# Projecting the values of one attention group with the weights stationary and turning them afterwards

## The chip, the cores and the metric

The kernel runs on one core of a Trainium2 chip. Times are device microseconds (us) of that core. Engines are called as in the profile: PE (TensorE, its weight loads shown apart as PEld), DVE (VectorE), ACT (ScalarE), POOL (GpSimd) and SP (SyncE, whose queue here issues the DMAs).

## What is computed

One layer of a hybrid trunk on 512 tokens of width 1024: a norm, one projection `w_in` that feeds four mixers (pooling, dilated attention, stick-breaking attention, an S5 state space branch), gates, an output projection, and a gated feed-forward layer. The change touches dilated attention, which has three groups of four heads of 64; group `g` attends among tokens at distance 1, 4 and 16:

```
proj = rmsnorm(x, g) @ w_in                       # [512, ...]
for g, (window, dil) in enumerate(((128, 1), (512, 4), (2048, 16))):
    # tokens r, r + dil, r + 2 dil, ... form a subsequence of their own
    s = q @ k.T / 8 + bias[bucket(distance)]      # banded, causal, per subsequence
    m = max(s); p = exp(s - m); den = sum(p)
    o[g] = (p @ v) / den;  lse[g] = m + log(den)
y = sum(softmax(lse over g)[g] * o[g])
```

In group 1 (dilation 4) there are four subsequences of 128 tokens. The product `p @ v` of one of them wants its 128 tokens of `v` on the partitions, with the head dimension along the row.

## The kernel before

Everything is kept transposed, features on the 128 partitions and the 512 tokens along the row. Each fp32 operand of a large product is split into a rounded high part and a remainder (`split`, and `split_next` for weights), and a product takes three matmuls: high by high, high by low, low by high.

The work is one main stream of products, written out in the order in which PE gets it, with weight chunks that are loaded on SP's queue (`load_next`), split in halves by ACT and DVE (`split_next`, one chunk ahead of its use) and then multiplied. Two forms of product occur. `mm3` holds a 128 x 128 block of weights stationary and moves all 512 tokens past it; eight k tiles by three make 24 matmuls, and the result is transposed (features on partitions). `act_stationary` holds 128 tokens of the input stationary and moves 256 columns of weights, again 24 matmuls; its result has the tokens on the partitions.

The projections of dilated attention are made in a loop over `g` = 0, 1, 2: queries, keys, values, two heads' worth (128 features) at a time for queries and keys. Tokens of groups 1 and 2 are put in the order of their subsequences when PSUM is evicted (`perm_out`, `perm_in`). For the values, groups 0 and 1 use `act_stationary` on four blocks of tokens: 128 neighbours in group 0, every fourth token, `slice(b, T, 4)`, in group 1. ACT evicts with the norm's per-token scale, a column: `rc[0]`, or `rc[1]`, the same scale in group 1's token order, which is made by a store to DRAM and a load back. Group 2 uses `mm3` twice, evicts on DVE with a permuting write into two `vf` tiles, and turns them later, in `dil_gen`, by eight 128 x 128 transposes on PE into two PSUM tiles `vt` and copies by ACT.

Everything else of the mixers is side work: generators (`s5_gen`, `dil_gen`, `sb_gen`, `pool_gen` and so on) that `start` puts on a list. `tick`, called after each product of the main stream, goes through the list and issues one step of each, in the order of the list. The list pauses a step where a simple account of engine times (`clock`) has DVE or ACT more than `MAX_LAG` = 4 us behind PE. PSUM has three banks for the main stream and five for side work, each in rotation. The order on every engine is thus fixed when the program is built. Around the values of group 1 the steps are: an S5 step and a step of scores after each half of the values, with the split of the next chunk (group 2's queries) before them; then group 2's queries, before which the chunk of its keys is split.

The lines that matter in the program: the loop `for g in range(3)` of the projections, `act_stationary`, `dil_gen`, and

```
if g < 2:
    vt = [slot("v"), slot("v")]
    for b in range(4):
        ps = main_ps("v")
        act_stationary(ps, ch, slice(b * P, (b + 1) * P) if g == 0 else slice(b, T, 4))
```

Of the kernel before, what the change touches and what calls it, by code (L numbers as in the profile page):

```python
# [10 lines left out]
F32 = mybir.dt.float32  # L11
F32R = mybir.dt.float32r
I32 = mybir.dt.int32
AF = mybir.ActivationFunctionType
ALU = mybir.AluOpType
AX = mybir.AxisListType
PSUM = bass.MemoryType.PSUM
DRAM = bass.MemoryType.DRAM

P = 128  # L20
T = 512
# [22 lines left out]
CST_CNT = 512  # L44
CST_W = CST_CNT + 64

N_SLOTS = 61  # [128, 512] tiles in the rotating pool
N_RAW = 2  # weight chunks loaded ahead
N_PM = 3  # PSUM banks of the main stream; the rest serve side work
S5_RATE = 0.9  # steps of the S5 branch per tick  # L50
SB_RATE = 1.0  # steps of the stick-breaking branch per tick
MAX_LAG = 4.0  # backlog of DVE and ACT (us) at which side work pauses
H_WAIT = 4  # ticks between the S5 rotation tables and their use
SB_T = 2  # steps from stick-breaking scores to their transposes
SB_O = 2  # steps from the transposes to the outputs
DIL_O = 1  # the same for the dilated branch
N_WARM = 8  # products on constants that bring up the PE clock while the first loads run
N_HALVED = 2  # last tiles of w_down done by token halves
BC_AT = 7  # k tiles of the last product before the first half is broadcast
W0_PIECES = {0: 1, 1: 3, 4: 2, 6: 2}  # first k tile: number of k tiles, pieces of the first weight chunk  # L60
S5_PAR = 48
S5_W = S5_PAR + 4 * 256

# [25 lines left out]
def hybrid_trunk(ctx: ExitStack, tc: tile.TileContext, a: dict, out: bass.AP):  # L89
    nc = tc.nc  # L90
    G, SY = nc.gpsimd, nc.sync
    clock = {"pe": 0.0, "v": 0.0, "a": 0.0}
# [12 lines left out]
    mixers = ExitStack()  # L105
# [9 lines left out]
    def slot(nm):  # L115
        return sp.tile([P, T], F32, tag="s", name=nm_(nm))
# [8 lines left out]
    def side_ps(nm):  # L125
        return pa.tile([P, T], F32, tag="at", name=nm_("s_" + nm))
# [9 lines left out]
        V.tensor_tensor(r_(lo), src, hi, ALU.subtract)  # L136
        return r_(hi), r_(lo)

    # ------------------------------------------------------- weight stream
    specs = (  # L140
        [("w_in", 17 + c, 2048) for c in range(2)]
        + [("w_in", 2 + 3 * w + g, 2048) for g in range(3) for w in range(3)]
# [21 lines left out]
    loaded, ready = [], []  # L164
# [35 lines left out]
            PE.matmul(ps, wh, al, start=False, stop=False)  # L200
            PE.matmul(ps, wl, ah, start=False, stop=k == n - 1)

    # ------------------------------------------------- side work scheduling
    active = []

    def start(gen, rate=1.0):
        active.append([gen, 0, rate, 0.0])
        return active[-1]
# [19 lines left out]
        while e in active:  # L228
            tick(True)

    # ---------------------------------------------------------------- loads
    ones = gp.tile([P, P], F32, name="ones")
    G.memset(ones, 1.0)
    warm = gp.tile([P, 1], F32, name="warm")
# [45 lines left out]
    def g3(kt):  # L280
        return cols[:, 16 + kt : 17 + kt]

    # ------------------------------------------------------------- rms norm
    def sumsq_add(acc, src):
        sq = slot("sq")
        A.activation(sq, src, AF.Square)
# [5 lines left out]
    def inv_rms(ps, n):  # L292
        def s_(nm):
            return gp.tile([P, n], F32, name=nm_(nm))

        ms = s_("ms")
        V.tensor_scalar(ms, ps, 1.0 / D, EPS, ALU.mult, ALU.add)
        rt = s_("rt")
        A.activation(rt, ps, AF.Sqrt, scale=1.0 / D, bias=epsc)
        r0 = s_("r0")  # L300
        V.reciprocal(r0, rt)
        t = s_("nt")
        V.tensor_tensor(t, r0, r0, ALU.mult)
        V.scalar_tensor_tensor(t, t, -0.5, ms, ALU.mult, ALU.mult)
        r = s_("rr")
        V.scalar_tensor_tensor(r, t, 1.5, r0, ALU.add, ALU.mult)
        return r

    def diags(r, nm):
        o = []  # L310
        for b in range(4):
            dg = sm.tile([P, P], F32, tag="dg", name=nm_("dg"), bufs=4)
            V.tensor_scalar(dg, ident, r[:, b : b + 1], None, ALU.mult)
            o.append(dg)
        return o
# [7 lines left out]
    def ssq_mm(acc):  # L323
        ps = side_ps("ssq")
        for b in range(4):
            PE.matmul(ps[:, b : b + 1], acc[:, b * P : (b + 1) * P], ones[:, 0:1], start=True, stop=True)
        return ps

    # ------------------------------------------------------------- prologue
    xg = []  # L330
    ch0 = Chunk()
    ch0.hi = wp.tile([P, 2048], F32R, tag="hi", name=nm_("hi"))
# [12 lines left out]
    rb8 = slot("rb8")  # L345
    env = {}

    # ------------------------------------------------- relative bias tables
    bias_d = dp.tile([12, BIAS_N], F32, name="bias_d")
    bias = {}  # L350

# [28 lines left out]
                SY.dma_start(bias[g, h], bass.AP(src.tensor, src.offset + off, [[1, P], [1, w]]))  # L380
            off += BIAS_L[g]

    # -------------------------------------------------------- S5 parameters
    s5 = cp.tile([P, S5_W], F32, name="s5p")
    are, aim, ldt = s5[:, 0:16], s5[:, 16:32], s5[:, 32:48]

# [287 lines left out]
            ys5.append(split(yg, "yg"))  # L674
            yield

    # ------------------------------------------------------ dilated attention
    def perm_out(t, g):
        if g == 0:
            return t  # L680
# [33 lines left out]
    def dil_score(g, hp, bl):  # L714
# [14 lines left out]
        for hh in range(2):  # L729
# [15 lines left out]
                )  # L745
            yield

    def dil_gen():
        for g in range(3):
            while len(dk) < 2 * g + 2:  # L750
# [3 lines left out]
                    yield from dil_score(g, hp, bl)  # L754
            if g:
                move(stat_d[g], stats[g].rearrange("p b s h -> p b (s h)"), g, True)
        vt = [slot("v"), slot("v")]
        for hb in range(2):
            ps = side_ps("vt")
            for bb in range(2):  # L760
                b = 2 * hb + bb
                for n in range(2):
                    PE.transpose(ps[:, bb * 256 + n * P : bb * 256 + n * P + P], vfs[n][:, b * P : (b + 1) * P], ident)
            A.copy(vt[hb], ps)
        dv.append(vt)
        yield
        for g in (1, 2):
            move(stat_d[g], nat[g].rearrange("p b s h -> p b (s h)"), 0, False)
        yield 2
# [73 lines left out]
                    V.tensor_scalar(st[:, o : o + kn], st[:, o : o + kn], fw[g][:, b, h : h + 1], None, ALU.mult)  # L843
            yield

    # ------------------------------------------------------- stick breaking
    sq, sk, sv = [], [], []
    m_up = cst[:, CST_UP : CST_UP + P]
    m_low = cst[:, CST_LOW : CST_LOW + P]
# [44 lines left out]
                V.tensor_tensor(be[:, : n - 1], be[:, : n - 1], om[:, 1:n], ALU.mult)  # L894
            yield

    # ----------------------------------------------------------------- pool
    ypool = [None] * 4
    pwt = []

# [33 lines left out]
        V.scalar_tensor_tensor(r_(lo), ps, cols[:, 24 + g : 25 + g], hi, ALU.mult, ALU.subtract)  # L934
        ypool[g] = (r_(hi), r_(lo))

    # ------------------------------------------------------------ main: w_in
    start(bias_tables())
    start(pool_load())
    e_s5 = start(s5_gen(), S5_RATE)  # L940
# [23 lines left out]
            split_next()  # L964
    ch = next_chunk()
    mm3(pss[2], ch, 0, 256, xg)
    rc = [inv_rms(ssq_mm(acc)[:, 0:4], 4), gp.tile([P, 4], F32, name="rc_perm")]
    dgs = diags(rc[0], "r1")
    rc_d = dp.tile([T], F32, name="rc_d")
    SY.dma_start(rc_d.rearrange("(b p) -> p b", b=4), rc[0])  # L970
    SY.dma_start(rc[1], rc_d.rearrange("(p b) -> p b", b=4))
    mm3(pss[3], ch, P, 256, xg)
    bcast_rows(dgs, rb)
    V.tensor_scalar(rb8, rb, 0.125, None, ALU.mult)
# [5 lines left out]
    def act_stationary(ps, ch, tk):  # L980
        for k, (ah, al) in enumerate(xg):
            PE.matmul(ps[:, 0:256], ah[:, tk], ch.h(k, 0, 256, 256), start=k == 0, stop=False)
            PE.matmul(ps[:, 0:256], al[:, tk], ch.h(k, 0, 256, 256), start=False, stop=False)
            PE.matmul(ps[:, 0:256], ah[:, tk], ch.l(k, 0, 256, 256), start=False, stop=k == KT - 1)

    e_dil = start(dil_gen())
    for g in range(3):
        for lst, scale in ((dq, rb8), (dk, rb)):
            ch = next_chunk()
            for n in range(2):  # L990
                ps = main_ps("qk")
                mm3(ps, ch, n * P, 256, xg)
                t = slot("qk")
                V.tensor_tensor(perm_out(t, g), perm_in(ps, g), perm_in(scale, g), ALU.mult)
                lst.append(t)
                tick()
        ch = next_chunk()
        if g < 2:
            vt = [slot("v"), slot("v")]
            for b in range(4):  # L1000
                ps = main_ps("v")
                act_stationary(ps, ch, slice(b * P, (b + 1) * P) if g == 0 else slice(b, T, 4))
                A.activation(
                    vt[b // 2][:, (b % 2) * 256 : (b % 2) * 256 + 256],
                    ps[:, 0:256],
                    AF.Copy,
                    scale=rc[g][:, b : b + 1],
                )
                if b % 2:
                    tick()  # L1010
            dv.append(vt)
        else:
            for n in range(2):
                ps = main_ps("v")
                mm3(ps, ch, n * P, 256, xg)
                t = slot("vf")
                V.tensor_tensor(perm_out(t, g), perm_in(ps, g), perm_in(rb, g), ALU.mult)
                vfs.append(t)
                tick()

    def sb_qk(c):
        for lst in (sq, sk):
# [9 lines left out]
    def sb_v(c):  # L1032
        ch = next_chunk()
        vt = [slot("sv"), slot("sv")]
        for b in range(4):
            ps = main_ps("sv")
            act_stationary(ps, ch, slice(b * P, (b + 1) * P))
            A.activation(
                vt[b // 2][:, (b % 2) * 256 : (b % 2) * 256 + 256], ps[:, 0:256], AF.Copy, scale=rc[0][:, b : b + 1]
            )  # L1040
            if b % 2:
                tick()
        sv.append(vt)
# [18 lines left out]
    sb_v(1)  # L1062
    e_sb = start(sb_gen(), SB_RATE)

    # --------------------------------------------------- gates and branches
    merged = [slot("mg") for _ in range(8)]
    mg = []

# [46 lines left out]
    branch(3, yglu, last=True)  # L1115
    mixers.close()

    # ------------------------------------------------- output of the mixers
    fp = ctx.enter_context(tc.tile_pool(name="ffn", bufs=1))

    def keep(nm):
# [18 lines left out]
            acc = sumsq_add(acc, t)  # L1140
    rb2 = keep("rb2")

    # ------------------------------------------------------------------ ffn
    def glu_up(psg, psu):
        tg, tu = slot("tg"), slot("tu")
        V.tensor_tensor(tg, psg, rb2, ALU.mult)
# [28 lines left out]
            if part:  # L1175
                acc = sumsq_add(acc, x2[nt])

    # ------------------------- the last tiles by token halves, final rms norm
    H = T // 2
    last = [(nt, next_chunk()) for nt in range(8 - N_HALVED, 8)]  # L1180
    pq = [side_ps("ssq"), side_ps("ssq")]
# [201 lines left out]
```

## Time and profile before

| | |
|---|---|
| median of 3 runs | 1000.56 us (1000.35 to 1001.05) |
| span of the profiled execution | 999.0 us |
| PE busy | 986.6 us (99%) |
| PEld busy | 828.5 us (83%) |
| DVE busy | 574.1 us (57%) |
| ACT busy | 361.5 us (36%) |
| DMA | 100.18 MB, mean 100 GB/s |

The page gives the span, from the first to the last instruction, of the one execution that was profiled, and no other time of it; the median is 1.56 us above it. Busy times overlap between engines. The records of all operations carry line 79, that of the helper which issues them, so instructions are told apart by the tiles that they write and read: `m_v` is the PSUM tile of a value projection, `s_vt` that of the transposes, `xh` and `xl` the two parts of the input, `hi` and `lo` those of a weight chunk. In "m_v<-hi,xh 128*128 128x256" the first operand moves, the second is stationary.

### The profile page before, as it was taken

The numbers are of one execution on the slowest core, as the hardware profiler recorded it, in microseconds if no ns is written. First come the engines' busy times: TensorE is split into PE (matmuls) and PEld (weight loads), VectorE is DVE, ScalarE is ACT, GpSimd is POOL, SyncE is SP. The second block draws the span as 40 slices with busy tenths as digits, with TensorE's granted clock in tenths as the row PEclk, the third lists the DMA queues.
The fourth block names the chain that finished last, engine by engine and source line by source line (L and its number), as shares of the span: only waits on it lengthen the run. The fifth ranks groups of instructions, "written<-read, shape, count | busy, mean of one in ns | idle before, by whom it ended". The sixth has DMA issues, their size and how long they took to land.

```text
span 999.0 us, 12492 instructions
## 1 busy us (share of the span) xinstructions
PE 986.6 (99%) x4926; PEld 828.5 (83%) x4926; DVE 574.1 (57%) x1108; ACT 361.5 (36%) x606; POOL 4.3 (0%) x20
## 2 busy tenths in 40 slices
PE   8999999999999999999999999999999999999996
PEld 7888988988988888887888888888888888888886
DVE  6576358578877877865635565445443244454344
ACT  6253344333445444226433343332222122232231
POOL 1000000000000000000000000000000000000000
PEclk9999999999999999999999999999999999999998
DMA  7442031422112213352352323222312323222212
GB/s 270 150 139 95 9 124 52 138 73 85 64 54 69 71 49 95 119 190 92 120 176 95 117 89 125 84 85 85 114 58 99 131 85 124 87 85 87 87 59 85
DMA packets 39362, 100.18 MB, mean 100 GB/s; under 512 B 14894, under 2 KB 22747, under 8 KB 33544
## 3 DMA queue, kind: packets, MB, share of 16 engines
q1 hardware_dynamic: 39304, 99.38, 29.1%
q8 instruction: 39, 0.64, 0.2%
q14 instruction: 19, 0.16, 0.1%
HBM read 94.94 MB, written 4.42 MB: 99 GB/s over the span
## 4 chain that ended last, share of the span: by engine, by line
PE 96%; DVE 2%; ACT 1%; DMA 1%; issue 0%; SPq 0%; DVEq 0%
PE m_g L79 16%; PE m_fg L79 12%; PE m_d L79 12%; PE m_fu L79 11%; PE m_b L79 7%; PE m_qk L79 7%; PE m_v L79 5%; PE m_sqk L79 4%; PE m_o L79 4%; PE m_u L79 3%; PE m_sv L79 2%; PE s_fu L79 1%; PE m_gb L79 1%; PE m_ga L79 1%; PE s_psy L79 1%; PE s_u L79 1%
## 5 line engine op out<-in xcount | busy, mean ns | idle before, releaser
L79 DVE TENSOR_TENSOR lo<-raw,hi 128x1024 fp32r<-128x1024 f32 (+4 forms) x192 | 194.5, 1053 | 47.0 <-ACT hi L79 46.0
L79 ACT CAST hi<-raw 128x1024 fp32r<-128x1024 f32 (+4 forms) x192 | 166.1, 913 | 65.3 <-PE m_d L79 41.5
L79 PE MATMUL m_g<-xh,hi 128*128 128x512 f32 x256 | 102.6, 401 | 0.0
L79 PE MATMUL m_g<-xh,lo 128*128 128x512 f32 x256 | 100.0, 391 | 0.3 <-DVE lo L79 0.3
L79 PE MATMUL m_g<-xl,hi 128*128 128x512 f32 x256 | 99.6, 389 | 0.0
L79 PE MATMUL m_d<-hh,hi 128*128 128x512 f32 (+1 forms) x198 | 72.5, 366 | 0.0
L79 PE MATMUL m_d<-hl,hi 128*128 128x512 f32 (+1 forms) x198 | 72.4, 365 | 0.0
L79 PE MATMUL m_d<-hh,lo 128*128 128x512 f32 (+1 forms) x198 | 72.3, 365 | 0.0
L79 PE MATMUL m_fg<-x2h,hi 128*128 128x512 f32 x176 | 68.6, 390 | 0.0
L79 PE MATMUL m_fg<-x2h,lo 128*128 128x512 f32 x176 | 68.5, 389 | 0.0
L79 PE MATMUL m_fg<-x2l,hi 128*128 128x512 f32 x176 | 68.5, 389 | 0.0
L79 DVE TENSOR_TENSOR tu<-m_fu,rb 128x512 f32<-128x512 f32 x20 | 13.8, 691 | 95.0 <-PE m_fu L79 95.0
L79 PE MATMUL m_fu<-x2h,hi 128*128 128x512 f32 x160 | 62.2, 389 | 0.0
L79 PE MATMUL m_fu<-x2l,hi 128*128 128x512 f32 x160 | 62.2, 389 | 0.0
L79 PE MATMUL m_fu<-x2h,lo 128*128 128x512 f32 x160 | 62.2, 389 | 0.0
L79 ACT ACTIVATE gt<-gt 128x512 f32<-128x512 f32 x32 | 20.2, 632 | 109.1 <-DVE gt L79 109.1
L79 PEld LDWEIGHTS m_g<-xh,lo 128*128 128x128 f32 x256 | 48.0, 188 | 11.2 <-DVE lo L79 1.0
L79 PEld LDWEIGHTS m_g<-xh,hi 128*128 128x128 f32 x256 | 48.1, 188 | 10.9 <-issue 1.0
L79 PEld LDWEIGHTS m_g<-xl,hi 128*128 128x128 f32 x256 | 48.1, 188 | 10.7 <-issue 1.0
L79 ACT CAST hh<-tu 128x512 fp32r<-128x512 f32 x22 | 13.7, 622 | 113.9 <-DVE tu L79 113.9
L79 DVE TENSOR_TENSOR x<-m_d,x 128x512 f32<-128x512 f32 (+1 forms) x18 | 11.4, 632 | 65.3 <-PE m_d L79 65.3
L79 PEld LDWEIGHTS m_d<-hh,lo 128*128 128x128 f32 x198 | 37.3, 189 | 6.0
(352 smaller groups left out, 2057.6 us busy)
## 6 DMA issues: line engine op xcount, KB each, us to landing
raw<-in_w_up SPq DMA_DIRECT2D x22, 1024.0 KB, 4.7
raw<-in_w_g SPq DMA_DIRECT2D x24, 768.0 KB, 4.2
raw<-in_w_in SPq DMA_DIRECT2D x17, 1024.0 KB, 5.8
raw<-in_w_down SPq DMA_DIRECT2D x16, 704.0 KB, 4.0
raw<-in_w_g SPq DMA_DIRECT2D x8, 640.0 KB, 3.7
raw<-in_w_out SPq DMA_DIRECT2D x4, 1024.0 KB, 4.7
x<-in_x SPq DMA_DIRECT2D x8, 256.0 KB, 4.6
raw<-in_w_glu SPq DMA_DIRECT2D x2, 1024.0 KB, 7.4
```

Of the source, the lines that this page charges most:

```text
L79: return f(out, *args, **kw)
```

## The change

Group 1's values are made as group 2's are: `mm3` with the weights stationary, all 512 tokens moving, a permuting eviction by DVE into two `vf` tiles, and eight transposes on PE with two copies by ACT. The transposes of both groups are now in a generator `v_gen(g)`; group 1's is started as side work right behind the projection, group 2's runs inside `dil_gen` where its code stood. The scale in group 1's token order, `rc[1]`, is gone with its store and load; `rc` is the one that was `rc[0]`. The comments on the constants were taken out too.

```
+    def v_gen(g):
+
+        vt = [slot("v"), slot("v")]
+        for hb in range(2):
+            ps = side_ps("vt")
+            for bb in range(2):
+                b = 2 * hb + bb
+                for n in range(2):
+                    o = bb * 256 + n * P
+                    PE.transpose(ps[:, o : o + P], vfs[2 * g - 2 + n][:, b * P : (b + 1) * P], ident)
+            A.copy(vt[hb], ps)
+        dv.append(vt)
+        yield
+
     def dil_gen():
...
-        vt = [slot("v"), slot("v")]
-        for hb in range(2):
-            ps = side_ps("vt")
-            for bb in range(2):
-                b = 2 * hb + bb
-                for n in range(2):
-                    PE.transpose(ps[:, bb * 256 + n * P : bb * 256 + n * P + P], vfs[n][:, b * P : (b + 1) * P], ident)
-            A.copy(vt[hb], ps)
-        dv.append(vt)
-        yield
+        yield from v_gen(2)
...
-    rc = [inv_rms(ssq_mm(acc)[:, 0:4], 4), gp.tile([P, 4], F32, name="rc_perm")]
-    dgs = diags(rc[0], "r1")
-    rc_d = dp.tile([T], F32, name="rc_d")
-    SY.dma_start(rc_d.rearrange("(b p) -> p b", b=4), rc[0])
-    SY.dma_start(rc[1], rc_d.rearrange("(p b) -> p b", b=4))
+    rc = inv_rms(ssq_mm(acc)[:, 0:4], 4)
+    dgs = diags(rc, "r1")
...
-        if g < 2:
+        if g == 0:
             vt = [slot("v"), slot("v")]
             for b in range(4):
                 ps = main_ps("v")
-                act_stationary(ps, ch, slice(b * P, (b + 1) * P) if g == 0 else slice(b, T, 4))
+                act_stationary(ps, ch, slice(b * P, (b + 1) * P))
                 A.activation(
                     vt[b // 2][:, (b % 2) * 256 : (b % 2) * 256 + 256],
                     ps[:, 0:256],
                     AF.Copy,
-                    scale=rc[g][:, b : b + 1],
+                    scale=rc[:, b : b + 1],
                 )
                 if b % 2:
                     tick()
...
                 V.tensor_tensor(perm_out(t, g), perm_in(ps, g), perm_in(rb, g), ALU.mult)
                 vfs.append(t)
                 tick()
+            if g == 1:
+                start(v_gen(1))
```

## Rows read from the trace of the kernel before

**Rows 1.** The page, part 1: engine, busy us (share of span), instructions.

```profile
span 999.0 us, 12492 instructions
PE 986.6 (99%) x4926; PEld 828.5 (83%) x4926; DVE 574.1 (57%) x1108; ACT 361.5 (36%) x606; POOL 4.3 (0%) x20
```

**Rows 2.** Waits of PE, two of five: who for whom, total us, times, longest.

```profile
PE s_u L79 <- ACT hi L79: 2.2, 2, 1.9
...
PE m_g L79 <- DVE lo L79: 0.3, 1, 0.3
```

**Rows 3.** The chain of waits in order of time: start us, us, what.

```profile
57.15 11.71 PE m_v L79 x96
...
95.55 11.41 PE m_v L79 x48
107.07 11.21 PE m_v L79 x48
118.28 1.09 PE s_sc L79 x16
...
131.57 11.11 PE m_qk L79 x48
...
145.55 11.10 PE m_v L79 x48
...
168.86 0.88 PE s_vt L79 x8
...
625.63 5.44 PE m_fg L79 x24
```

**Rows 4.** Tiles by form, groups 0, 1, 2: ns min/median/max, starts, shapes.

```profile
L79 PEld LDWEIGHTS m_v<-hi,xh x32: 186/192/193, 57.1 to 68.2; 128*128 128x128 f32 x32
...
L79 PEld LDWEIGHTS m_v<-hi,xh x32: 309/329/332, 95.5 to 117.3; 128*128 128x128 f32 x32
...
L79 PE MATMUL s_vt<-cst,vf x8: 270/272/273, 168.7 to 169.5; 128*128 128x128 f32 x8
```

**Rows 5.** Stretches: us, PE, PEld, DVE, ACT, POOL busy (x), PEclk, DMA, GB/s.

```profile
95.48:118.21 22.73, 22.73 (x100) 22.60 (x98) 9.01 (x28) 5.49 (x14) 0.00 (x0) 1.00 0.03 4
104.57:106.90 2.33, 2.33 (x13) 2.33 (x12) 2.25 (x7) 0.00 (x0) 0.00 (x0) 1.00 0.00 0
```

**Rows 6.** PE in order of time at group 1's values: start us, us.

```profile
95.48 0.51 PE L79 MATMUL m_v<-hi,xh 128*128 128x256 f32 x1
...
106.56 0.40 PE L79 MATMUL m_v<-lo,xh 128*128 128x256 f32 x1
...
107.15 0.40 PE L79 MATMUL m_v<-hi,xl 128*128 128x256 f32 x1
...
118.21 1.16 PE L79 MATMUL s_sc<-qk,qk 64*128 64x128 f32 x16
```

**Rows 7.** ACT on the values' tile, by form: ns min/median/max, starts.

```profile
L79 ACT ACTIVATE v<-m_v,rc_perm x4: 473/474/474, 101.4 to 118.3; 128x256 f32<-128x256 f32 x4
L79 ACT COPY v<-s_vt x2: 566/572/579, 170.0 to 170.5; 128x512 f32<-128x512 f32 x2
```

**Rows 8.** SP's queue: a wait, its order of time, page's part 6.

```profile
SPq L971 <- DMA rc_d<-rr: 7.8, 1, 7.8
...
109.11 14.04 SPq L604 DMA_DIRECT2D mt<-k_d  x20
...
raw<-in_w_in SPq DMA_DIRECT2D x17, 1024.0 KB, 5.8
```

**Rows 9.** DVE and ACT in order of time, idle time before in brackets.

```profile
93.08 1.09 DVE L79 TENSOR_TENSOR qk<-m_qk,rb 128x512 f32<-128x512 f32 x1 [0.79 <-PE m_qk L79]
...
119.40 0.29 DVE L79 CUSTOM_DVE_ANT_0 prob<-s_sc,bias 128x128 f32<-128x128 f32 x1 [12.51 <-PE s_sc L79]
...
124.86 1.99 ACT L79 CAST hi<-raw 128x1024 fp32r<-128x1024 f32 x2
125.92 2.36 DVE L79 TENSOR_TENSOR lo<-raw,hi 128x1024 fp32r<-128x1024 f32 x2 [5.38 <-ACT hi L79]
```

More of the change, by code (lines that the diff above doesn't have):

```diff
@@ L1038, in sb_v @@
             A.activation(
-                vt[b // 2][:, (b % 2) * 256 : (b % 2) * 256 + 256], ps[:, 0:256], AF.Copy, scale=rc[0][:, b : b + 1]
+                vt[b // 2][:, (b % 2) * 256 : (b % 2) * 256 + 256], ps[:, 0:256], AF.Copy, scale=rc[:, b : b + 1]
             )
```

## The prediction, made before the result was known

> **What bounds the kernel now.** I read the page's first part first, because it says which engine to count on. TensorE (PE) is busy for 986.6 of the 999.0 us of the span, VectorE (DVE) for 574.1 [rows 1]. A busy PE is not yet a bound, since the profile models the ends of its matmuls, so the second view is what PE waited for. That list has five rows and 5.9 us in all; the longest and the shortest stand in [rows 2], and the other three are of 1.0 to 1.4 us, at the kernel's start or end. So PE is fed nearly throughout, and the time of the kernel is the sum of what its instruction stream takes. The third view is the chain of waits in order of time. In the stretch of the change it names nothing but PE: group 0's values take 11.71 us for 96 matmuls, group 1's 11.41 + 11.21 us for as many of the same shape, and group 2's 11.10 us for 48 of 512 columns [rows 3]. All three do the same arithmetic. The middle one costs twice the others, and that is what the change touches.
>
> Why it costs twice is read from the matmul tile by form. In group 0 the weight load takes 192 ns in the median, in group 1 it takes 329 ns; shape, type and count are the same [rows 4]. What differs in the code is the stationary operand: four-byte values one after another in group 0, every fourth one in group 1. The matmuls with them start 11.21 / 48 = 0.234 us apart, against 11.71 / 96 = 0.122 us. [...]
>
> [...]
>
> **What is removed.** On PE, the block of 96 matmuls. Its first starts at 95.48, and the next other work in the stream, the scores after it, at 118.21 [rows 6]: 22.73 us, as the window that is cut there says too [rows 5]. One S5 transpose sits inside and stays: around it the starts are 107.15 - 106.56 = 0.59 us apart [rows 6], two steps of 0.234 are 0.47, so it is worth 0.12. On ScalarE (ACT), four scaled copies of 474 ns go, 1.90 us [rows 7]. On the queue of SyncE (SP), the two small transfers of the permuted row scale go; the second blocked the queue for 7.8 us while it waited for the first [rows 8]. Behind it stood four stores of S5 inputs, two loads of small weights and the next weight chunks. They can move forward by a few us at most; PE waits for nothing there, so I count nothing, and if I am wrong it is a gain under 1 us.
>
> **What is added.** On PE, 48 matmuls with the weights stationary. They are group 2's block over again, which takes 11.10 us [rows 3]. With the S5 transpose inside it is 11.22. From below, two halves at the 5.44 us that 24 such matmuls take in a stretch without side work [rows 3], and 0.12, give 11.0; from above, a pace like the old one's 0.234 gives 48 x 0.234 + 0.12 = 11.35. I take 11.22, the row of the same operation.
>
> Eight transposes of 128 x 128 come on top. The eight that group 2 already has lengthen the chain by 0.88 us [rows 3]. Sixteen other small matmuls take 1.09 us, which would make eight 0.55 [rows 3]; eight that didn't overlap would take 8 x 272 ns = 2.18 [rows 4]. I take 0.88, the same operation in the same kernel. They are issued by a side step of their own, entered last in the list of active ones, so they land behind the first half of group 2's queries; no step of another branch gives up its tick for them.
>
> On DVE come two evictions with a permuting write. The same write on group 1's keys takes 1.09 us [rows 9], so 2.18 us. On ACT come two copies of 572 ns, 1.14 us [rows 7], less than the 1.90 removed. They can queue behind the exponentials of the scores; the readers of these values are products that come behind the softmax over all three groups, so only the two PSUM banks are held longer. There are five side banks, used in turn, and by the order of the steps the next tenants of these two come a whole projection later, behind the next pair of score tiles; I count nothing.
>
> **The sum.** 22.73 - 11.22 - 0.88 = 10.63 us less on PE. The span of the profiled execution is 999.0 and becomes 988.4. The median of the runs is 1000.56, 1.56 more, and I take that to be what lies around the span and to stay: 1000.56 - 10.63 = **989.9 us**.
>
> **What is late next.** The half as long block takes cover away from the side engines. DVE has 9.01 us of work in it [rows 5] and gets 2.18 more, in 11.22 us in place of 22.73. Before, it had caught up and then sat idle for 12.51 us, until the scores [rows 9]; that idle time is what the change spends. Followed in order (second eviction once PE is through at 106.8, 1.09 us, then the last of the S5 angles, which fill the 2.33 us from 104.57 now [rows 5], then the scores), DVE reaches the scores about 3.4 us after the block's end, where before it did so 1.2 us after [rows 6, 9], so about 2.2 us later. The first thing that this could reach on PE is the split of the next weight chunk, group 2's keys. Before, it was done at 125.92 + 2.36 = 128.28 [rows 9], 10.07 us after the block's end, and the product that needs it started at 131.57 [rows 3], 13.36 after. Now the first number is some 12.3 and the second, with the transposes in between, 14.2: a margin of 1.9 us, and more for the first half of the chunk, which is what the product reads first. If DVE falls behind by another 2.3 us, as much as those angles, PE waits some 0.5 us. The chunk after it is loaded behind 20 small S5 transfers, which hold SP's queue for 14.04 us from 109.11 [rows 8]. These follow a copy that comes some 6 us earlier than now, while PE is 11 us earlier, so that load loses 5 us of its lead. It would be issued near 109.11 + 14.04 - 6 = 117; the chunk is wanted near 145.55 - 10.6 = 135 [rows 3], and takes 5.8 us to land [rows 8] and 3.4 to split, from 124.86 to 128.28 [rows 9]. That holds. From there on every branch moves with the ticks of the main stream, so I expect the rest of the trace to be shifted and not changed.
>
> **The rivals.**
> - The lost cover shows. DVE and ACT fall behind, and PE waits at group 2's keys or values. For it speaks that DVE is nearly full in the new block (11.2 of 11.2 us); against it the margin of 1.9 us above and the idle DVE afterwards. If the weight chunk came no earlier by the clock than now, PE would wait until 127.1 (125.92 + half of 2.36) for its first half, having been ready at 120.9, a loss of 6.2; a likely size is 1 to 3 us. Time 991 to 993, at the extreme 996. Chance 0.07.
> - The transposes don't overlap and cost their 272 ns each: 989.9 + 1.3 = 991.2. Against it is the 0.88 us of the chain. Chance 0.03.
> - It is no matter of the stride: group 0's 11.71 us is the true cost of the old block, and something of that stretch doubled it that stays. Then 11.22 + 0.88 - 11.71 = 0.4 us are lost, 1001.0. Against it, the load is 329 ns from the first to the last of 96 (309 to 332 in all), with DVE busy and with DVE idle. Chance 0.02.
> - The other side, by one mechanism: the bound in this stretch is not PE but the chain from DVE's evictions over ACT's exponentials to the split of the chunk, and PE only looks busy. Then the two evictions on DVE, 2.18 us, are simply added: 1002.7. The split is done 8.9 us after DVE reaches the scores (10.07 - 1.2), so PE begins to wait when DVE is 5.4 us behind at the block's end, and the change turns into a loss at 16.0; I get 3.4, and the 12.51 us of idle DVE speak against any. Chance 0.02.
> - What is won is given back later, at a point timed by transfers and not by PE: the S5 branch, which is timed in part by its small transfers [rows 8]; the one wait of PE for a weight split, 0.3 us [rows 2], falls where its last steps crowd ACT. Its loads and tables would have to keep their old time, and then 1000.6. Against it, all its steps are issued by ticks of the main stream. Chance 0.02.
>
> **How the numbers follow.** Forecast as computed 0.84. Its own bounds: the block 11.0 to 11.35, the transposes 0.55 to 2.18, and some 1 us either way for edges and waits that I haven't found, 988.4 to 991.3. The range is drawn out to 992.3 to take in most of the first rival; below, to 988.3. What a measurement can tell from no change is about 0.2%, 2 us. Faster by more than that: 0.84 + 0.07 + 0.03, nothing of the rest, 0.94. Within it: 0.02 for the stride and 0.02 for what is given back, 0.04. Slower: 0.02.
>
> **What would show it.** In the trace after: 48 matmuls of 512 columns into the values' tile with weight loads of about 188 ns where 96 with 329 were; about 11.2 us from the first to the scores behind them; eight more transposes, 0.9 us, between the halves of group 2's queries; no new row of over 0.5 us among PE's waits; DVE's idle time before the scores gone, down to under 1 us. The forecast is wrong if PE waits for a weight split near 121 or 135, or if the 48 matmuls run at a slower pace than group 2's.

## The result, and the profile after

The changed kernel takes 988.84 us (median of 4, 988.42 to 990.60), the kernel before 1000.70 us in the same runs: a ratio of 0.9888, with a 95% interval of 0.9874 to 0.9902. That is faster by 11.9 us. Timed again on another chip, beside the kernel before, it took 988.83 against 999.70 us: 10.9 us, ratio 0.9887 (0.9870 to 0.9904). The forecast was 10.63 us less, 989.9.

The page after, part 1, answers to [rows 1]:

```profile
span 986.6 us, 12413 instructions
PE 973.9 (99%) x4886; PEld 814.2 (83%) x4886; DVE 576.1 (58%) x1110; ACT 360.5 (37%) x604; POOL 4.3 (0%) x20
```

PE has 40 instructions fewer (96 matmuls gone, 48 and 8 come) and is still 99% busy: it bounds the kernel as before. DVE has two more, the two evictions.

The chain of waits after, in order of time (start us, us, what), answers to [rows 3]:

```profile
94.01 5.67 PE m_v L79 x24
99.68 0.11 PE s_psk L79
99.79 5.47 PE m_v L79 x24
105.26 1.09 PE s_sc L79 x16
106.35 5.67 PE m_qk L79 x24
112.03 0.87 PE s_vt L79 x8
112.90 5.49 PE m_qk L79 x24
118.39 1.09 PE s_sc L79 x16
119.48 5.67 PE m_qk L79 x24
```

The block of group 1's values is two halves of 24 with the S5 transpose of 0.11 us between, 11.25 us in all from 94.01 to 105.26, where 22.73 stood. The new transposes sit between the halves of group 2's queries and cost 0.87. There is nothing but PE in the chain, so nothing new became the bound.

The values' tile by form, in the changed kernel (ns min/median/max, first and last start), answers to [rows 4]:

```profile
L79 PEld LDWEIGHTS m_v<-xh,hi x16: 186/188/189, 93.9 to 104.2; 128*128 128x128 f32 x16
L79 PE MATMUL m_v<-xh,hi x16: 389/389/497, 93.9 to 104.4; 128*128 128x512 f32 x16
...
L79 DVE TENSOR_TENSOR vf<-m_v,rb x2: 1054/1074/1094, 99.7 to 105.3; 128x512 f32<-128x512 f32 x2
```

The loads are the ordinary ones of 188 ns; the 329 ns of [rows 4] are gone. The evictions take 1.05 to 1.09 us each, where 1.09 was read from group 1's keys.

PE's waits after, which answer to [rows 2] (who for whom, total us, times, longest):

```profile
PE s_u L79 <- ACT hi L79: 2.6, 2, 1.4
...
PE s_u L79 <- DVE lo L79: 0.3, 1, 0.3
PE m_g L79 <- DVE lo L79: 0.3, 1, 0.3
```

Three of the six rows; the first two are of the start-up, before 10 us, and the last was there before. In the stretch of the change no wait for a weight split has come.

DVE and ACT after, in order of time around the end of the block, answer to [rows 9]:

```profile
105.30 1.05 DVE L79 TENSOR_TENSOR vf<-m_v,rb 128x512 f32<-128x512 f32 x1 [0.94 <-PE m_v L79]
106.20 0.67 DVE L79 SCALAR_TENSOR_TENSOR ang<-kt,ang 128x512 f32<-128x512 f32 x1
...
108.42 0.28 DVE L79 CUSTOM_DVE_ANT_0 prob<-s_sc,bias 128x128 f32<-128x128 f32 x1
...
113.30 1.99 ACT L79 CAST hi<-raw 128x1024 fp32r<-128x1024 f32 x2
114.36 2.36 DVE L79 TENSOR_TENSOR lo<-raw,hi 128x1024 fp32r<-128x1024 f32 x2 [4.81 <-ACT hi L79]
```

The scores' row has no bracket: the 12.51 us of idle DVE are spent. The split of group 2's keys is through at 116.72, 2.8 us before the product that needs it.

**Where the 12.4 us of the two profiled spans went.** Group 1's values begin at 95.48 before [rows 6] and, by PE's order of time, at 93.94 after: 1.54 us are won before the change has done anything on PE. They are won in the first 20 us: the product into `m_u` begins at 20.49 before and at 18.94 after, and from there to group 1's values the two streams take the same time. The granted clock of the first 30 us shows it. The same stretch in the kernel before, and then in the changed one (us, busy times, clock, DMA share, GB/s):

```profile
0.00:30.00 30.00, 26.77 (x110) 21.77 (x111) 18.67 (x31) 19.01 (x28) 4.28 (x20) 0.94 0.64 225
```

```profile
0.00:30.00 30.00, 26.20 (x117) 21.55 (x118) 19.15 (x32) 18.85 (x28) 4.28 (x20) 1.00 0.65 225
```

In the execution before, the first products of the kernel waited up to 1.9 us for a weight split and then ran at a granted clock of 0.50 (from 10 to 12 us; it is 1.00 again from 13 us on); in the one after they waited too, up to 1.4 us at a time, and the clock stayed at 1.00. The length of the wait alone doesn't decide it: with the transfers put back (below, the first of the two runs), a wait of 1.9 us left the clock at 1.00 too. The block and the transposes give 22.73 - 11.25 - 0.87 = 10.6, and 0.26 come at the very end, behind the last products.

### The profile page after: what moved, and what is told of

Same layout as the page of the kernel before. It is cut to its first block, busy times and chain, and to the rows that moved or that the text cites. A ratio compares the mean times of both kernels' runs of the same rounds, so it can differ in the third digit from the quotient of the medians.

```text
span 986.6 us, 12413 instructions
## 1 busy us (share of the span) xinstructions
PE 973.9 (99%) x4886; PEld 814.2 (83%) x4886; DVE 576.1 (58%) x1110; ACT 360.5 (37%) x604; POOL 4.3 (0%) x20
## 4 chain that ended last, share of the span: by engine, by line
PE 96%; DVE 2%; ACT 1%; DMA 1%; issue 0%; SPq 0%; DVEq 0%
PE m_g L79 17%; PE m_fg L79 12%; PE m_d L79 12%; PE m_fu L79 11%; PE m_b L79 7%; PE m_qk L79 7%; PE m_sqk L79 4%; PE m_o L79 4%; PE m_v L79 3%; PE m_u L79 3%; PE m_sv L79 2%; PE s_fu L79 1%; PE m_gb L79 1%; PE m_ga L79 1%; PE s_psy L79 1%; PE s_u L79 1%
## 5 line engine op out<-in xcount | busy, mean ns | idle before, releaser
L79 PEld LDWEIGHTS m_g<-xh,hi 128*128 128x128 f32 x256 | 48.1, 188 | 10.9 <-issue 1.0
L79 PEld LDWEIGHTS m_d<-hh,hi 128*128 128x128 f32 x198 | 37.3, 189 | 6.1
```

Source lines behind the costliest of these rows:

```text
L79: return f(out, *args, **kw)
```

## The experiments

The theory: a weight load whose values lie four apart is the whole of what the old block lost. Rivals: the 256-column form or the number of loads costs it; the removed transfers matter; the cover that the old block gave to DVE is missed.

**Neighbouring tokens in the old form.**

```diff
-    act_stationary(ps, ch, slice(b * P, (b + 1) * P) if g == 0 else slice(b, T, 4))
+    act_stationary(ps, ch, slice(b * P, (b + 1) * P))
```

> The kernel before, with group 1's stationary blocks taken as 128 neighbouring tokens (so group 1's values are those of other tokens). Still 96 matmuls of 256 columns, no transposes. If the stride of four in the weight load is the whole cost: weight loads fall from 329 to about 192 ns, the block from 22.73 to 11.71 + 0.12 = 11.8 us, the kernel by 10.9 us, to some 989.7, 0.3 us below what the 48 matmuls and eight transposes should give. If the number of weight loads or the place in the stream is the cost: loads stay at 329 ns, block near 22.7, time as before. If half the cost is the 256-column form: block between, 16 to 18 us.

Measured: 988.86 us (988.31 to 990.49), ratio to the kernel before 0.9881 (0.9865 to 0.9898). Its tile by form and its chain:

```profile
L79 PEld LDWEIGHTS m_v<-hi,xh x32: 186/192/192, 94.3 to 105.6; 128*128 128x128 f32 x32
```

```profile
94.39 5.95 PE m_v L79 x48
100.34 0.11 PE s_psk L79
100.45 5.75 PE m_v L79 x48
106.20 1.09 PE s_sc L79 x16
```

With the form and the number of matmuls kept and only the step taken away, the load is back at 192 ns and the block at 11.81 us. The step was the cost, all of it. The time is 12.2 us under the median of the kernel before on that chip, 1.3 more than expected; four of the seven runs of the kernel before there have a mean clock of 0.995 and take 1001.0 to 1002.0, the three of 0.996 and 0.997 take 999.9 to 1000.1, so the block in the trace is the surer figure. That block also prices what the change pays for its detour: 11.25 + 0.87 is 0.3 us more than this block. In the totals that difference is below the spread of the runs.

**Steps of two, three and eight.** The first two slice the tokens as shown; the third reads every eighth value of the weight chunk, since 128 values eight apart don't fit in 512 tokens.

```diff
# abridged, group 1 only; the step of eight is a loop over the k tiles
-    slice(b, T, 4)
+    slice(b // 2 * 256 + b % 2, b // 2 * 256 + 256, 2)        # step of two
+    slice(b, b + 384, 3)                                      # step of three
+    slice(2 * b + 128 * k, 2 * b + 128 * k + 1017, 8)         # step of eight, of ch.hi and ch.lo
```

> The kernel before, with every second token in group 1's stationary blocks (values of other tokens). [...] Theory B, any step but one costs the same: load 329 ns, block 22.7. Theory C, cost grows with the step: near 240 ns, block 14 to 17 us.

> [...] Theory B (any step but one): 329 ns, 22.7 us. Theory C (grows with the step): about 285 ns, 18 us. [...]

> The kernel before, with group 1's stationary blocks read from the weight chunk itself, every eighth value of its 2048 (so group 1's values are not the reference's); 96 matmuls of 256 columns as before. Steps 1, 2, 3, 4 gave loads of 192, 195, 262, 329 ns and starts 0.122, 0.122, 0.179, 0.234 us apart. [...]

Measured, one run each: 990.07, 995.89 and 1001.67 us. The loads by form, steps of two, three and eight in this order:

```profile
L79 PEld LDWEIGHTS m_v<-hi,xh x32: 194/195/200, 95.7 to 107.0; 128*128 128x128 f32 x32
```

```profile
L79 PEld LDWEIGHTS m_v<-hi,xh x32: 250/261/267, 95.8 to 112.3; 128*128 128x128 f32 x32
```

```profile
L79 PEld LDWEIGHTS m_v<-hi x32: 312/337/340, 95.2 to 117.6; 128*128 128x128 f32 x32
```

And the second half of the block in the chain, in the same order:

```profile
101.82 5.77 PE m_v L79 x48
```

```profile
104.56 8.54 PE m_v L79 x48
```

```profile
107.14 11.53 PE m_v L79 x48
```

So 48 matmuls take 5.75, 5.77, 8.54, 11.21 and 11.53 us at steps of one, two, three, four and eight; per matmul 0.120, 0.120, 0.178, 0.234 and 0.240. A step of two is free here, from there the time grows up to a step of four, and a step of eight adds 0.006 us to that. Theory B misses with a step of two, 0.120 us a matmul and 195 ns a load, where four apart takes 0.234 us and 329 ns. Theory C misses with it too: a load of 195 ns where it had 240, a half block of 5.77 us where it had 7 to 8.5. Nor does the time go by the distance that the values cover: eight apart cover twice that of four, in 0.240 against 0.234 us. What in the load makes these times is not shown.

**The step on the moving side.** The tokens are permuted on the way into the array, and evicted straight; four apart, which gives the same values as the change, and two apart.

```diff
# abridged, group 1 only
-    mm3(ps, ch, n * P, 256, xg)
+    # pr: "p (l r) -> p r l", rl: "p (r l) -> p r l", r = 4 or 2
+    mm3(rl(ps), ch, n * P, 256, [(pr(ah), pr(al)) for ah, al in xg])
+    V.tensor_tensor(rl(t), rl(ps), pr(rb), ALU.mult)
```

> The changed kernel, with the tokens of group 1's values permuted on the way into the array, the 512 moving columns read with a step of four values (16 bytes), and evicted without permuting. The sum of the results is the same. If the moving side suffers from the step as the stationary side does (about 0.234 us for 128 values): 512 columns take up to 0.9 us, block 48 x 0.45 to 0.9 = 22 to 45 us, kernel 1000 to 1022. If only weight loads suffer: 0.227 us apart as now, block 11.25, kernel as the changed one, with DVE's two evictions down from 1.07 to about 0.7 to 1.07 us each.

> As the run with strided moving columns, with a step of two values (8 bytes) in place of four; group 1's values come out in another token order than the reference's. A step of four doubled the matmul, 0.461 us for 512 columns. [...] If the cost is in proportion: 0.30 to 0.35 us, block 15 to 17.

Measured: 999.28 and 1000.05 us. In the chain, the second half of the block, 24 matmuls, four apart and then two apart:

```profile
105.05 11.07 PE m_v L79 x24
```

```profile
105.51 10.83 PE m_v L79 x24
```

0.461 and 0.451 us for a matmul that takes 0.228 with neighbouring columns. Four apart is at the lower end of what was expected, about 0.9 ns a column, and throws the whole gain away. Two apart was a miss: it is not in proportion, and costs nearly as much as four. So a step of two is free on the stationary side, 0.120 us a matmul as with neighbours, and on the moving side it is not. One rival is left here: the moving operand, and the result with it, is also written as a pattern of two levels, and no run has such a pattern with neighbouring values.

**The step in the transposes.** Values are evicted in token order, and the transposes read every fourth column as their stationary operand.

```diff
-    V.tensor_tensor(perm_out(t, g), perm_in(ps, g), perm_in(rb, g), ALU.mult)
+    V.tensor_tensor(t, ps, rb, ALU.mult)                                       # g == 1
...
-    PE.transpose(ps[:, o : o + P], vfs[2 * g - 2 + n][:, b * P : (b + 1) * P], ident)
+    PE.transpose(ps[:, o : o + P], vfs[2 * g - 2 + n][:, b:T:4], ident)        # g == 1
```

> The changed kernel, with group 1's values evicted in token order and the transposes reading every fourth token as their stationary operand. The 48 matmuls don't change. If a strided weight load costs the same here as in the old block: the eight loads rise from 140 to about 280 to 330 ns, their stretch from 0.88 to 1.9 to 2.2 us, kernel slower by 1.0 to 1.3 us, evictions 1.07 to 0.69 us each. If the fp32 transposes load by another path that doesn't mind the step: stretch stays 0.88 us, time unchanged.

Measured: 989.42 us, one run. Tile by form, then the chain:

```profile
L79 PEld LDWEIGHTS s_vt<-cst,vf x8: 197/209/209, 112.1 to 113.0; 128*128 128x128 f32 x8
```

```profile
112.50 0.95 PE s_vt L79 x8
```

Between the two expectations: the loads rise from 140 to 209 ns, but the stretch only from 0.87 to 0.95 us. In this plain fp32 transpose a stationary operand read four apart costs at most some 0.12 us (0.95 / 8), half of the 0.234 us a matmul that it cost in the rounded fp32r products of the block. Why is open. The evictions fall to 0.69 us each, and as DVE has room, nothing is won by that.

**More work on DVE.** The second eviction of group 1's values is repeated, twice and six times.

```diff
+    if g == 1 and n == 1:
+        for _ in range(2):        # or 6
+            nc.vector.tensor_tensor(perm_out(t, g), perm_in(ps, g), perm_in(rb, g), ALU.mult)
```

> The changed kernel, with the second eviction of group 1's values made three times in place of once: some 2.0 us more on DVE just where its cover is least. By the trace of the changed kernel the split of group 2's keys is through with its first half 3.9 us before the product reads it. Theory: hidden, no new wait of PE, block, transposes and time as the changed kernel. Rival (DVE's chain is the bound of the stretch): PE waits 2 us at the start of group 2's keys.

> As the run before with six more evictions in place of two: some 6.1 us on DVE. Theory: past the cover of 3.9 us, so PE waits some 2.2 us (1.5 to 3) for the split of group 2's keys, and the kernel loses as much. Rivals: hidden altogether (0), or added in full (6).

Measured: 988.55 and 991.02 us on the same chip, spans of 986.8 and 989.2. With two more, PE's list of waits gains no row. With six more it gains three; the rows of that run which belong to this stretch:

```profile
PE s_vt L79 <- DVE vf L1022: 1.0, 1, 1.0
...
PE m_qk L79 <- DVE lo L79: 0.5, 1, 0.5
PE m_qk L79 <- ACT hi L79: 0.4, 1, 0.4
```

PE in order of time there, at the product of group 2's keys:

```profile
121.22 0.50 PE L79 MATMUL m_qk<-xh,hi 128*128 128x512 f32 x1 [0.43 <-ACT hi L79]
...
122.47 0.50 PE L79 MATMUL m_qk<-xh,lo 128*128 128x512 f32 x1 [0.53 <-DVE lo L79]
```

The product starts at 121.22, where it starts at 119.57 in the run with two more, and then stops once more. The three waits come to 1.9 us, and the span is 2.4 us longer; the half us of difference stands in no row. The size is near the 2.2 that were expected, but the split of the keys makes up only 1.0 of it: the other 1.0 is a wait that I had not foreseen, of the transposes for the repeated evictions themselves. The cover is there, and it is finite: two microseconds more on DVE are free, six are not.

**The transfers put back**, with nobody reading the permuted scale; run twice, the second time on one chip with the changed kernel.

```diff
# abridged
+    SY.dma_start(rc_d.rearrange("(b p) -> p b", b=4), rc)
+    SY.dma_start(rc_p, rc_d.rearrange("(p b) -> p b", b=4))
```

> The changed kernel with the two small transfers of the permuted row scale put back (nobody reads their result). The measured gain is 11.9 us, the block and the transposes give 10.6 to 10.9. Theory: the transfers are worth nothing, and the rest is the start-up before 30 us, which differs from run to run by its clock: time as the changed kernel's, 988.4 to 990.6, with the spread following the mean clock. Rival: freeing the queue of SP of its 7.8 us wait is worth the missing 1 us: 989.8 or more in the runs of high clock.

> The changed kernel with the two row-scale transfers, on the same chip as the run before. Theory (they are worth nothing): same time as the changed kernel within 0.5 us. Rival (so far all five profiles with the transfers reach group 1's values later, at 95.2 in the mean against 94.1 for the five without, but on different chips): 1 us slower.

> The changed kernel, again, beside the kernel before and beside the one with the row-scale transfers put back, on the same chip. The block and the transposes give 10.6 to 10.9 us. Theory (start-up differs by chance, from chip to chip and run to run): first matmul of group 1's values between 93.6 and 95.9 in either kernel, gain 10.5 to 12.

Measured: first 989.64 us (989.35 to 990.65), on a chip where no changed kernel ran. Then 989.21 (989.10 to 989.34) beside 988.83 (988.43 to 989.38) for the changed kernel. These two differ by 0.4 us, inside the changed kernel's own spread, so the totals don't settle it. The traces do. From the first product of group 0's values to the first of group 1's, PE takes 38.4 us in all seven profiled executions without the transfers, and in the three with them that had a late start-up (clock 0.94: the kernel before, steps of two and three). In the other four with them it takes 38.75 (neighbouring tokens), 38.81 and 38.86 (the two runs here) and 39.66 us (step of eight). Two executions with the same start-up show why: the one with moving columns four apart (no transfers, the product into `m_u` begun at 18.62 us) and the second run here (18.61). ACT in order of time, in the first and then in the second:

```profile
44.65 2.00 ACT L79 CAST hi<-raw 128x1024 fp32r<-128x1024 f32 x2 [4.52 <-DMA raw<-in_w_in]
...
62.25 0.82 ACT L79 ACTIVATE v<-m_v,rr 128x256 f32<-128x256 f32 x2
```

```profile
48.57 2.00 ACT L79 CAST hi<-raw 128x1024 fp32r<-128x1024 f32 x2 [4.10 <-DMA raw<-in_w_in]
...
63.79 0.82 ACT L79 ACTIVATE v<-m_v,rr 128x256 f32<-128x256 f32 x2
```

And PE in the second, where the first has no wait:

```profile
64.31 0.39 PE L79 MATMUL m_v<-hi,xh 128*128 128x256 f32 x1 [0.20 <-ACT v L79]
```

Behind the transfers the next weight chunk is issued later (39.99 against 37.84 us) and lands later; its split, the side work that follows it and ACT's first evictions of group 0's values come later with it, and the last of these four products waits for them. Group 1's values then begin at 94.07 in place of 93.62. The rival is thus right in part: beside a good start-up the transfers cost PE 0.35 to 1.26 us, in four executions of four; beside a late one PE comes some 1.5 us later and meets no wait. Of the changed kernel's 10.9 us on this chip the block and the transposes are 10.6.

## Why the prediction was right

The place and the mechanism were read rightly, and each term of the sum on PE came out within 0.1 us. The block: 11.25 for 11.22. The transposes: 0.87 for 0.88, at the place in the stream that was named. The rest of the stream is shifted as expected: the S5 product after group 2 begins at 168.54 in place of 180.63, the first of the gated products of S5 at 482.94 in place of 495.07, both by 12.1 us, so nothing is given back in between.

What was late next was sized on the safe side. DVE reaches the scores 108.42 - 105.19 = 3.2 us after the block's end (3.4 predicted); the split of group 2's keys is done 11.5 us after it (12.3), the product starts at 14.3 (14.2). The margin is 2.8 us where I had 1.9, and 3.8 for the half that is read first. That the cover decides only beyond that is what the two runs with more evictions showed.

Of the rivals, the one that held the stride for innocent fell with the first experiment, the one with costly transposes with the 0.87 us, the one with a chain over DVE as the bound with the two evictions that cost nothing.

One term was put at nothing with a reason that holds for one execution alone: the transfers, since "PE waits for nothing there". In the execution that was read the start-up had made PE some 1.5 us late, and it did wait for nothing; in the four with the transfers and a good start-up they cost 0.35 to 1.26 us, one of them more than the "under 1 us" that was allowed for. So to a kernel before that starts well, removing them is a gain of its own. Two smaller things were off as well. The 0.3 us wait was called the only one for a weight split; the 2.2 us of [rows 2] are one too, at the start. And of the prediction's own bounds the lower, 988.4, has the 1 us for edges in it and the upper, 991.3, has not; added up alike, that is 992.4.

The forecast of 989.9 lies 1.1 us above the time measured first. The difference isn't in the block or the transposes, since those are right to 0.1 us in the traces. The span was to fall to 988.4 and fell to 986.6: 1.54 us of this are the start-up, before anything that the change touches on PE, and 0.26 the end. Against it, a run takes 1.75 to 1.92 us more than its span in the four timed runs of the changed kernel, where 1.56 had been taken from a span and a median of different executions. The range reached down to 988.3; that the total stayed within it, by 0.5 us, rests in part on how the start-ups fell.

In eleven of the fourteen executions profiled here the first 30 us have a granted clock of 1.00, and the product into `m_u` begins between 18.61 and 19.42 us; in the kernel before and in the runs with steps of two and three the clock is 0.94, and it begins between 20.49 and 20.86. The timed runs of the changed kernel fit: the one of 990.60 has a mean clock of 0.994, the other three, 988.42 to 989.02, of 0.996 and 0.997. So a part of the 11.9 us is likely a start-up that happened to be better, and the 10.9 us of the second chip, 0.2 from the forecast, the fairer figure. That the start-up falls by chance and not with the kernel is not shown: of the seven executions with the transfers of the row scale three had it at 0.94, of the seven without none. But the transfers are issued only at 28 to 30 us, behind the stretch in which the clock falls (8 to 13 us in the kernel before), and of the pair on the second chip the run with the transfers had the better start-up, 18.61 us against 19.07.

## What to carry to other kernels

Where PE bounds the kernel, read the weight loads by form: a load that is far longer than its neighbours of the same shape and type (329 against 192 ns) was here a stationary operand read with a step, and it set the pace of its matmuls. Here a step of two was free for the stationary side (0.120 us a matmul, as with neighbours), while both steps tried on the moving side doubled the matmul (0.451 and 0.461 us against 0.228); for values four apart, a contiguous product and eight transposes of 0.11 us were cheaper than a step on either side of the product. Before such a block is halved, count what the other engines did under it, and how far they were ahead: here 12.5 us of idle DVE paid for it, with 2.8 us to spare. And "PE waits for nothing there", read from one execution, can be the mark of a late start-up: a wait can appear as soon as PE comes earlier.

## What the runs showed that I had not expected

- A step of two on the moving side costs as much as one of four: 0.451 and 0.461 us for 512 columns, against 0.228.
- A plain fp32 transpose hardly minds a step of four in its stationary operand: eight in 0.95 us against 0.87, where the pace of the rounded products went from 0.120 to 0.234 us a matmul.
- The start-up differs between executions by up to 2.25 us (the product into `m_u` begins between 18.61 and 20.86), more than the finest effects studied here.
- Two small transfers in SP's queue, at 28 us, cost PE 0.35 to 1.26 us some 35 us later, but only where the start-up was good.
